# Order of the expert loop: gate products before linear products, a two-part activation, output products before the branch

## The chip, the cores and the metric

The kernel runs as one program on one core of a Trainium2 chip. The metric is the device time of one execution in microseconds (us). The median of three runs of the kernel before is 1742.16 us (1737.1 to 1744.37).

Five engines of the core work side by side, each with its own instruction stream: PE (TensorE, matrix products; PEld is its loading of weights), DVE (VectorE), ACT (ScalarE), POOL (GpSimd) and SP (SyncE, which here issues the loads of weights). They wait for each other by semaphores. In an fp32 product the trace shows two matmul records and two weight loads for each matmul that the program writes.

## The reference

Two transformer blocks on 256 tokens of width 1024. The first block ends in a mixture of 32 experts, of which each token takes four. This part is what the change touches:

```python
def moe_ffn(h, w_router, b_router, w_gu, b_gu, w_dn, b_dn):
    logits = (h @ w_router + b_router).astype(jnp.float32)
    top_logits, top_e = lax.top_k(logits, TOP_K)
    top_w = jax.nn.softmax(top_logits, axis=-1).astype(h.dtype)
    ...
    def expert_block(args):
        xe, e = args
        gu = xe @ w_gu[e] + b_gu[e]
        x_glu = jnp.minimum(gu[:, :D_FF], SWIGLU_LIMIT)
        x_lin = jnp.clip(gu[:, D_FF:], -SWIGLU_LIMIT, SWIGLU_LIMIT)
        act = (x_lin + 1) * (x_glu * jax.nn.sigmoid(SWIGLU_ALPHA * x_glu))
        return act @ w_dn[e] + b_dn[e]
    ...
    y = jnp.zeros((T + 1, D), h.dtype).at[slot_tok].add(yb.reshape(n_slots, D) * slot_w[:, None])
    return y[:T]
```

All arrays are float32. The weights of one expert are 12 MB (8 MB `w_gu`, 4 MB `w_dn`), all 32 experts 384 MB.

## The kernel before

**The loop.** The experts run one after the other (`for e in range(NX)`), 64 places (`CAP`) per expert. In the schedule written by hand, each engine does its instructions in the order of the code. One turn of the loop is, on PE:

1. `overflow(e)` (L1109 on): every engine loads the number of tokens of expert e (`TENSOR_LOAD`, L1121) and branches (`COMPARE_BRANCH`, L1122). If there are more than 64, an extra block `block(1)` does a whole expert for the next 64 tokens with the same weights; a second branch (L1124) guards two more. In the run traced here only expert 17 takes the extra block. Else PE jumps over all three blocks.
2. `up` (L1052): the bias by a product with `btab` (L1057), then for each of 8 tiles of `w_gu` (k = 0 to 7, 1 MB each) two products into the gate's accumulator `pg` and two into the linear part's `pl` (L1062). Two products of 64 columns each run beside each other. The tile is then free (`ring.done`). The activation follows on DVE and ACT: `g = min(pg, 7)` (L1069), `s = sigmoid` on ACT (L1070), and `a` from `pl`, `g` and `s` in three steps on DVE (L1071 to L1073).
3. `pre_gather(e + 1)`: 48 small products (L1028) collect the next expert's tokens in `px`; ACT copies them to `xe` (L1031).
4. Two of the four output products of the last pair of experts (`scatter_steps`, L1101, `po` from `sw` and `yb`; DVE adds each to `y`, L1103). Two experts fill the two halves of one `yb`.
5. For odd e `turn_weights` (L1047): four transposes that turn the slot weights `pw`; DVE copies them to `sw` (L1049).
6. `turn_act` (L1076): four transposes of `a` into `pa` (L1079), and one copy on ACT to `aT` (L1081).
7. `down` (L1084): the bias (L1088), then 16 products of `aT` with the four tiles of `w_dn` (L1092) into `py`. For odd e, ACT and DVE copy `py` to `yb` (L1176).

**The loads.** Class `Ring` holds a list of all weight tiles in order of use (12 per expert) and a set of buffers of 1 MB. SP issues the load of a tile into the buffer that was freed first (L68). Eight semaphores tell of the landings in turn, so that eight loads at most are under way.

**Buffers.** `pg`, `pl`, `sw`, `aT`, `yb` and `py` have one buffer each, `ps_x` (for `px`, `pw`, `pa`) and `ps_o` (for `po`) two.

## Time and profile before

| | |
|---|---|
| median of three runs | 1742.16 us |
| the profiled execution | 1738.1 us, of which the span of the trace 1736.4 us |
| PE busy | 1564.3 us (90% of the span) |
| PEld busy | 953.9 us (55%) |
| DVE busy | 662.1 us (38%) |
| ACT busy | 440.2 us (25%) |
| POOL busy | 135.6 us (8%) |
| read from HBM | 529.19 MB, 306 GB/s over the span |
| mean granted clock of TensorE | 0.957 of full speed |

The experts begin at 321.87 us of the span and their last `down` ends at 1315.8 us; what stands before makes the routing, what comes behind is the second block. A time in the text is counted from the start of the span. The granted clock has two levels, 1.00 (2.4 GHz) and 0.5 (1.2 GHz); a figure between them is a mean over a stretch. A busy share is a mean over stages with different limits; what holds the experts is read from rows of the experts.

### The profile page before, as it was taken

To read this page: it belongs to the slowest core of one execution; us is meant where nothing else is said; L and a number is where in the kernel's file an instruction comes from. 1 tells how busy PE (TensorE), PEld (TensorE's weight loads), DVE (VectorE), ACT (ScalarE), POOL (GpSimd) and SP (SyncE) were. 2 spreads that over 40 slices of the span, in tenths; PEclk is the share of its full clock that TensorE was granted. 3 is DMA by queue.
4 is the path that set the end of the run, shared out by engine and by line. 5 is a ranking of instruction groups with operands and counts; after the bars stand their busy time and mean duration, and the time that the engine had idled before them with its cause. 6 is when DMAs were issued, how large, how long until landed. Compare 5 with 4: busy or idle time off the path is not lost. (4 is left out here: it accounts for less than half of the span.)

```text
span 1736.4 us, 25332 instructions
## 1 busy us (share of the span) xinstructions
PE 1564.3 (90%) x10281; PEld 953.9 (55%) x10281; DVE 662.1 (38%) x1336; ACT 440.2 (25%) x940; POOL 135.6 (8%) x186
## 2 busy tenths in 40 slices
PE   5999998689898889989898988989887999999997
PEld 2887778433333233333233333333344989899996
DVE  3656567312121121212122121212116676766665
ACT  3445444200000000000000000000003666455554
POOL 3125012100000000000000000000003300200000
PEclk8999999699999899999999999999988999999999
DMA  9725867799999999999599999999973544455552
GB/s 366 173 93 204 303 236 290 287 416 416 416 417 415 418 414 417 416 416 417 220 400 417 416 397 417 415 416 417 416 292 99 189 146 146 132 171 194 173 199 91
DMA packets 163434, 533.79 MB, mean 307 GB/s; under 512 B 15957, under 2 KB 84758, under 8 KB 127264
## 3 DMA queue, kind: packets, MB, share of 16 engines
q1 hardware_dynamic: 159986, 523.56, 77.8%
q0 software_dynamic: 2480, 6.79, 1.2%
q8 instruction: 146, 2.39, 0.6%
q10 hardware_dynamic: 766, 0.60, 0.1%
q14 instruction: 56, 0.46, 0.1%
HBM read 529.19 MB, written 1.71 MB: 306 GB/s over the span
## 5 line engine op out<-in xcount | busy, mean ns | idle before, releaser
L1062 PE MATMUL pge<-ring,xee 128*64 128x512 f32 x1024 | 305.3, 633 | 8.6 <-issue 8.6
L1062 PE MATMUL ple<-ring,xee 128*64 128x512 f32 x1024 | 303.3, 629 | 1.0 <-issue 1.0
L1069 DVE TENSOR_SCALAR ge<-pge 128x512 f32<-128x512 f32 x32 | 22.1, 692 | 638.5 <-issue 617.6
L393 DVE TENSOR_TENSOR wlo<-ring,whi 128x512 fp32r<-128x512 f32 x338 | 215.7, 698 | 78.6 <-ACT whi L390 77.2
L1092 PE MATMUL py<-ring,aTe 128*64 128x512 f32 x1024 | 226.8, 595 | 12.6 <-ACT aTe L1081 7.9
L1070 ACT ACTIVATE se<-ge 128x512 f32<-128x512 f32 x32 | 20.2, 631 | 689.3 <-DVE ge L1069 689.3
L390 ACT CAST whi<-ring 128x512 fp32r<-128x512 f32 x344 | 188.2, 620 | 23.2 <-issue 17.8
L1062 PEld LDWEIGHTS ple<-ring,xee 128*64 128x64 f32 x1024 | 97.1, 145 | 146.5 <-issue 141.6
L1062 PEld LDWEIGHTS pge<-ring,xee 128*64 128x64 f32 x1024 | 97.1, 145 | 141.0 <-issue 125.4
L1092 PEld LDWEIGHTS py<-ring,aTe 128*64 128x64 f32 x1024 | 70.7, 137 | 150.0 <-issue 125.1
L1057 PE MATMUL pge<-btab,pick 96*64 96x512 bf16 x64 | 14.4, 403 | 80.6 <-PEq L1122 70.1
L1133 POOL DMA_DIRECT2D gains<-mod_dr x1 | 0.6, 604 | 932.0 <-DMA ring<-in_w_gu_dram 932.0
L1028 PEld LDWEIGHTS <-parts 128*128 128x128 bf16 x1584 | 49.1, 99 | 29.3 <-PE pge L1062 25.2
L1057 PEld LDWEIGHTS <-pick 96*64 96x64 bf16 x132 | 5.7, 107 | 107.9 <-issue 67.9
L1101 PE MATMUL poe<-yb,swe 128*128 128x512 f32 x128 | 62.8, 614 | 0.7 <-ACT yb L1176 0.7
L1028 PE MATMUL pxe<-onee,parts 128*128 128x64 bf16 x1536 | 51.5, 195 | 3.2 <-DVE rs L995 3.2
L1176 DVE COPY yb<-py 128x512 f32<-128x512 f32 x16 | 11.1, 692 | 105.7 <-PE py L1092 105.7
L443 PE MATMUL ua<-h3l,whi 128*128 128x256 f32 x176 | 49.9, 284 | 0.7 <-DVE h3l L1266 0.7
L444 PE MATMUL ua<-h3h,wlo 128*128 128x256 f32 x176 | 49.9, 284 | 0.0
L442 PE MATMUL ua<-h3h,whi 128*128 128x256 f32 x176 | 49.8, 283 | 0.0
L444 PE MATMUL uv<-h3h,wlo 128*128 128x256 f32 x176 | 49.2, 280 | 0.0
L442 PE MATMUL uv<-h3h,whi 128*128 128x256 f32 x176 | 49.1, 279 | 0.0
(581 smaller groups left out, 2960.7 us busy)
## 6 DMA issues: line engine op xcount, KB each, us to landing
ring<-in_w_gu_dram SPq DMA_DIRECT2D x256, 1024.0 KB, 15.7
ring<-in_w_dn_dram SPq DMA_DIRECT2D x128, 1024.0 KB, 16.4
ring<-in_w_in_dram SPq DMA_DIRECT2D x37, 1024.0 KB, 5.5
ring<-in_w_mod_dram SPq DMA_DIRECT2D x24, 1024.0 KB, 7.4
ring<-in_w_up_dram SPq DMA_DIRECT2D x22, 1024.0 KB, 5.0
ring<-in_w_down_dram SPq DMA_DIRECT2D x11, 1024.0 KB, 4.8
ring<-in_w_o_dram SPq DMA_DIRECT2D x4, 1024.0 KB, 7.3
ring<-in_w_out_dram SPq DMA_DIRECT2D x4, 1024.0 KB, 5.1
```

Source lines behind the costliest of these rows:

```text
L390: nc.scalar.copy(hq, wq)
L393: eng.tensor_tensor(out=lq, in0=wq, in1=hq.bitcast(F32), op=ALU.subtract)
L442: nc.tensor.matmul(ps, ah, bh, start=first, stop=False)
L443: nc.tensor.matmul(ps, ah, bl, start=False, stop=False)
L444: nc.tensor.matmul(ps, al, bh, start=False, stop=last)
L1028: nc.tensor.matmul(px[:, k, :], parts[:, t, q, k * P : (k + 1) * P], one[:, t, :], start=(t == 0 and q == 0 and k == 0), stop=(t == NT - 1 ...
L1057: nc.tensor.matmul((pg, pl)[ch // 2][64 * (ch % 2) : 64 * (ch % 2) + 64, :], sel, btab[:, ch * 512 : (ch + 1) * 512], start=True, stop=False)
L1062: nc.tensor.matmul((pg, pl)[ch // 2][64 * (ch % 2) : 64 * (ch % 2) + 64, :], xe[:, k, :], w[:, ch * 512 : (ch + 1) * 512], start=False, st ...
L1069: nc.vector.tensor_scalar_min(g, pg, 7.0)
L1070: nc.scalar.activation(out=s, in_=g, func=AF.Sigmoid, scale=1.702)
L1092: nc.tensor.matmul(at[c], aT[:, k % 4, 64 * (k // 4) : 64 * (k // 4) + 64], w[:, k % 2, c * 512 : (c + 1) * 512], start=False, stop=(k == ...
L1101: nc.tensor.matmul(po, sw[:, c, t * P : (t + 1) * P], yb[c], start=True, stop=True)
```

## The change

It changes the order of the expert loop; what is computed stays. In `up`, tiles 0 to 3 are used as before; tiles 4 to 7 are first used for the gate alone, then for the linear part, and are freed in this second pass. `g` is multiplied with `s` before the linear part is looked at, and the rest of the activation is done in two halves of 256 columns. `turn_act` transposes and copies each half by itself. The output products move from their place between `pre_gather` and `turn_act` to the end of the turn, behind `down` and so ahead of the next branch. `turn_weights` moves from the odd expert to the even one behind it, `slot_weights` behind it. In the extra block, the slot weights are computed and turned before the activation.

```diff
-        for k in range(KD):
+        def products(k, chunks):
             w = ring.get(("gu", e, k))
-            for ch in range(4):
+            for ch in chunks:
                 nc.tensor.matmul((pg, pl)[ch // 2][64 * (ch % 2) : 64 * (ch % 2) + 64, :], xe[:, k, :], w[:, ch * 512 : (ch + 1) * 512],
                                  start=False, stop=(k == KD - 1))
-            if release:
+            if release and 3 in chunks:
                 ring.done(("gu", e, k))
+        for k in range(KD // 2):
+            products(k, range(4))
+        for chunks in ((0, 1), (2, 3)):
+            for k in range(KD // 2, KD):
+                products(k, chunks)
...
         nc.scalar.activation(out=s, in_=g, func=AF.Sigmoid, scale=1.702)
-        nc.vector.tensor_scalar(out=a, in0=pl, scalar1=7.0, scalar2=-7.0, op0=ALU.min, op1=ALU.max)
-        nc.vector.scalar_tensor_tensor(out=a, in0=a, scalar=1.0, in1=g, op0=ALU.add, op1=ALU.mult)
-        nc.vector.tensor_tensor(out=a, in0=a, in1=s, op=ALU.mult)
+        nc.vector.tensor_tensor(out=g, in0=g, in1=s, op=ALU.mult)
+        for c in (slice(0, 256), slice(256, 512)):
+            nc.vector.tensor_scalar(out=a[:, c], in0=pl[:, c], scalar1=7.0, scalar2=-7.0, op0=ALU.min, op1=ALU.max)
+            nc.vector.scalar_tensor_tensor(out=a[:, c], in0=a[:, c], scalar=1.0, in1=g[:, c], op0=ALU.add, op1=ALU.mult)
...
-        for j in range(4):
-            nc.tensor.transpose(pt[:, j, :], a[:, j * P : (j + 1) * P], ident)
         aT = mp.tile([P, 4, P], F32, tag="aT", name=f"aT{name}", bufs=1)
-        nc.scalar.copy(aT, pt)
+        for c in range(2):
+            for j in (2 * c, 2 * c + 1):
+                nc.tensor.transpose(pt[:, j, :], a[:, j * P : (j + 1) * P], ident)
+            nc.scalar.copy(aT[:, 2 * c : 2 * c + 2], pt[:, 2 * c : 2 * c + 2])
...
         def block(b):
             name = f"v{e}_{b}"
-            aT = turn_act(up(e, gather(e, b, name), name), name)
+            xe = gather(e, b, name)
+            slot_weights(pw[1], e, b, (0, 2))
+            a = up(e, xe, name)
+            sw = turn_weights(pw[1], name)
+            aT = turn_act(a, name)
             py = ps_o.tile([P, 512], F32, tag="o", name=f"py{name}")
             down(e, aT, [py[64 * c : 64 * c + 64, :] for c in range(2)])
-            slot_weights(pw[1], e, b, (0, 2))
             yb = mp.tile([P, 512], F32, tag="ybv", name=f"yb{name}")
             nc.scalar.copy(yb, py)
-            scatter(turn_weights(pw[1], name), [yb, yb], name)
+            scatter(sw, [yb, yb], name)
...
     for e in range(NX):
-        odd = e % 2
+        odd, last_one = e % 2, e == NX - 1
         overflow(e)
 
-        one = select(e + 1, 0, f"e{e + 1}") if e + 1 < NX else None
-        if odd:
-            slot_weights(pw[0], e, 0, (1,))
+        one = None if last_one else select(e + 1, 0, f"e{e + 1}")
+        if odd or not e:
+            slot_weights(pw[0], e, 0, (1,) if odd else (0, 2))
         act = up(e, xs_.pop(e), f"e{e}", release=True)
 
-
         pre_gather(e + 1, one)
-        next(spread, None)
-        next(spread, None)
-        if odd:
+        if last_one:
+            run(spread)
             sw = turn_weights(pw[0], f"e{e}")
-        if e == NX - 1:
+        elif not odd and e:
+            sw = turn_weights(pw[0], f"e{e}")
+            spread = scatter_steps(sw, yb, f"e{e}")
+        act_T = turn_act(act, f"e{e}")
+        if not odd and e:
+            slot_weights(pw[0], e, 0, (0, 2))
+        if last_one:
             last_tables()
-        act_T = turn_act(act, f"e{e}")
-        if odd and e + 1 < NX:
-            slot_weights(pw[0], e + 1, 0, (0, 2))
-        if e == NX - 1:
             ring.pump()
...
         down(e, act_T, [py[c][rows[c], :] for c in range(2)], release=True)
+
+        next(spread, None)
+        next(spread, None)
         if odd:
             yb = [mp.tile([P, 512], F32, tag=f"yb{c}", name=f"yb{e}_{c}") for c in range(2)]
             for c in range(2):
                 (nc.scalar.copy, nc.vector.tensor_copy)[c](yb[c], py[c])
-            spread = scatter_steps(sw, yb, f"e{e}")
+    spread = scatter_steps(sw, yb, f"e{e}")
```

On PE, the end of expert 6's turn before (`py` is what `down` writes, `ring` a weight tile):

```order
L1092 MATMUL py_0_7843<-ring_7124,aTe_7841 64x512
L1092 MATMUL py_1_7844<-ring_7124,aTe_7841 64x512
L1092 MATMUL py_0_7843<-ring_7124,aTe_7841 64x512
L1092 MATMUL py_1_7844<-ring_7124,aTe_7841 64x512
L1121 TENSOR_LOAD counts
L1122 COMPARE_AND_BRANCH
```

and the same place of PE with the change (`poe` is an output product, `yb` and `swe` the last pair's outputs and turned slot weights):

```order
L1101 MATMUL py_0_7921<-ring_7195,aTe_7910 64x512
L1101 MATMUL py_1_7922<-ring_7195,aTe_7910 64x512
L1110 MATMUL poe_7949<-yb_0_7302,swe_7907 128x512
L1110 MATMUL poe_7952<-yb_1_7303,swe_7907 128x512
L1133 TENSOR_LOAD counts
L1134 COMPARE_AND_BRANCH
```

Two output products of 128 columns now stand between the last products of `down` and the branch; this holds from expert 2's turn on.

On PE, the products of `up` of expert 6 for tiles 4 to 7 before (`pge` the gate's accumulator, `ple` the linear part's):

```order
L1062 MATMUL pge_7717<-ring_6602,xee_7189 64x512 x2
L1062 MATMUL ple_7718<-ring_6602,xee_7189 64x512 x2
L1062 MATMUL pge_7717<-ring_7088,xee_7189 64x512 x2
L1062 MATMUL ple_7718<-ring_7088,xee_7189 64x512 x2
L1062 MATMUL pge_7717<-ring_7094,xee_7189 64x512 x2
L1062 MATMUL ple_7718<-ring_7094,xee_7189 64x512 x2
L1062 MATMUL pge_7717<-ring_7100,xee_7189 64x512 x2
L1062 MATMUL ple_7718<-ring_7100,xee_7189 64x512 x2
```

and with the change:

```order
L1062 MATMUL pge_7787<-ring_6656,xee_7260 64x512 x2
L1062 MATMUL pge_7787<-ring_7157,xee_7260 64x512 x2
L1062 MATMUL pge_7787<-ring_7163,xee_7260 64x512 x2
L1062 MATMUL pge_7787<-ring_7169,xee_7260 64x512 x2
L1062 MATMUL ple_7788<-ring_6656,xee_7260 64x512 x2
L1062 MATMUL ple_7788<-ring_7157,xee_7260 64x512 x2
L1062 MATMUL ple_7788<-ring_7163,xee_7260 64x512 x2
L1062 MATMUL ple_7788<-ring_7169,xee_7260 64x512 x2
```

The last tile is touched three product pairs earlier, and four pairs of linear products stand behind its gate product.

On DVE, the activation of expert 6 before (`ae` is `a`, `se` is `s`):

```order
L1069 TENSOR_SCALAR ge_7771<-pge_7717 128x512
L1071 TENSOR_SCALAR ae_7773<-ple_7718 128x512
L1072 SCALAR_TENSOR_TENSOR ae_7773<-ae_7773,ge_7771 128x512
L1073 TENSOR_TENSOR ae_7773<-ae_7773,se_7772 128x512
L1103 TENSOR_TENSOR y<-poe_7830,y 128x512
```

and with the change:

```order
L1076 TENSOR_SCALAR ge_7841<-pge_7787 128x512
L1078 TENSOR_TENSOR ge_7841<-ge_7841,se_7842 128x512
L1080 TENSOR_SCALAR ae_7843<-ple_7788 128x256
L1081 SCALAR_TENSOR_TENSOR ae_7843<-ae_7843,ge_7841 128x256
L1080 TENSOR_SCALAR ae_7843<-ple_7788 128x256
L1081 SCALAR_TENSOR_TENSOR ae_7843<-ae_7843,ge_7841 128x256
L1049 COPY swe_7907<-pwe_7902 128x512
```

Behind the linear part's last product stand four instructions of 256 columns instead of three of 512. The built program holds one more wait: the transposes of the second half wait for ACT's copy of the first half out of the same tile `pa`.

## Rows read from the trace of the kernel before

**Rows 1.** Windows: us, busy by engine, granted clock, DMA share, GB/s.
```profile
439.30:800.06 360.76, 324.36 (x1920) 129.93 (x1921) 70.51 (x144) 25.18 (x42) 0.00 (x0) 0.95 1.02 416
469.03:497.56 28.53, 25.96 (x162) 10.83 (x163) 6.75 (x14) 2.39 (x4) 0.00 (x0) 1.00 1.02 417
557.75:585.80 28.05, 25.52 (x160) 10.39 (x160) 5.02 (x10) 1.81 (x3) 0.00 (x0) 1.00 1.02 416
893.50:1254.27 360.77, 325.38 (x1921) 133.27 (x1922) 70.57 (x144) 25.18 (x42) 1.16 (x2) 0.95 1.01 413
```
**Rows 2.** Waits of PE, 439.30 to 1254.27: us in total, times, longest.
```profile
PE pge L1057 <- PEq L1122: 57.4, 26, 2.4
```
**Rows 3.** Timeline of PE round one branch: start, us, instructions, idle before.
```profile
880.46 1.96 PE L1101 MATMUL poe<-yb,swe 128*128 128x512 f32 x4
...
884.03 7.09 PE L1092 MATMUL py<-ring,aTe 128*64 128x512 f32 x32 [0.39 <-ACT aTe L1081]
893.50 0.41 PE L1057 MATMUL pge<-btab,pick 96*64 96x512 bf16 x2 [2.38 <-PEq L1122]
```
**Rows 4.** Lines of branch and last products: ns min/median/max, first to last start, us.
```profile
L1121 PEldq TENSOR_LOAD <-counts x1: 311/311/311, 886.7 to 886.7; - x1
L1122 PEldq COMPARE_BRANCH  x32: 82/6046/6250, 317.6 to 1276.2; - x32
L1092 PE MATMUL py<-ring,aTe x22: 592/592/592, 886.2 to 890.5; 128*64 128x512 f32 x22
L1028 PE MATMUL pxe<-onee,parts x21: 242/242/242, 316.8 to 317.9; 128*128 128x64 bf16 x21
```
**Rows 5.** Windows: granted clock behind a branch and, last, behind a short gap.
```profile
893.50:897.50 4.00, 4.00 (x14) 1.60 (x16) 0.00 (x0) 0.00 (x0) 0.00 (x0) 0.57 1.00 416
...
1510.04:1514.00 3.96, 3.96 (x34) 3.96 (x35) 2.86 (x8) 2.19 (x6) 3.04 (x4) 1.00 0.78 258
```
**Rows 6.** Timeline: the short gap of the row before, in the second block.
```profile
1510.04 0.39 PE L442 MATMUL ps_w_gla_branch<-sg_hi,whi 128*128 128x256 f32 x1 [1.22 <-DVE tgg L814]
```
**Rows 7.** Timeline of PE, expert 14: linear part's end to `down`.
```profile
908.50 1.05 PE L1062 MATMUL ple<-ring,xee 128*64 128x512 f32 x4
...
914.02 7.09 PE L1092 MATMUL py<-ring,aTe 128*64 128x512 f32 x32 [0.40 <-ACTq L1122]
```
**Rows 8.** Timeline of ACT: a copy in expert 14, and one of 256 columns.
```profile
911.09 0.59 ACT L1031 COPY xee<-pxe 128x512 f32<-128x512 f32 x1 [0.95 <-PE pxe L1028]
...
1337.96 0.37 ACT L1309 COPY fx<-ps_fq 128x256 f32<-128x256 f32 x1 [1.41 <-PE ps_fq L444]
```
**Rows 9.** Loads of tile 7 of experts 17 and 31: issue, and landing behind.
```profile
L68 SPq DMA_DIRECT2D ring<-in_w_gu_dram x1: 327/327/327, 810.3 to 810.3; - x1
...
DMA to landing us min/median/max: 19.9/19.9/19.9
...
L68 SPq DMA_DIRECT2D ring<-in_w_gu_dram x1: 327/327/327, 1261.8 to 1261.8; - x1
...
DMA to landing us min/median/max: 19.0/19.0/19.0
```
**Rows 10.** The first load issued after the extra block's pause.
```profile
L68 SPq DMA_DIRECT2D ring<-in_w_gu_dram x1: 332/332/332, 867.1 to 867.1; - x1
```
**Rows 11.** Timeline of PE in expert 17's extra block.
```profile
841.09 1.03 PE L1062 MATMUL plv<-ring,xev 128*64 128x512 f32 x4
...
845.88 8.78 PE L1092 MATMUL pyv<-ring,aTv 128*64 128x512 f32 x32 [0.40 <-ACT aTv L1081]
...
856.13 3.87 PE L1101 MATMUL pov<-ybv,swv 128*128 128x512 f32 x8 [0.88 <-DVE swv L1049]
863.07 0.53 PE L1057 MATMUL pge<-btab,pick 96*64 96x512 bf16 x2 [3.08 <-PEq L1124]
```
**Rows 12.** Timeline of PE, expert 31: after its branch, and its `down`.
```profile
1287.99 0.59 PE L1057 MATMUL pge<-btab,pick 96*64 96x512 bf16 x1 [5.19 <-issue]
...
1308.69 7.09 PE L1092 MATMUL py<-ring,aTe 128*64 128x512 f32 x32 [0.40 <-ACT aTe L1081]
```

More of the change, by code (lines that the diff above doesn't have):

```diff
@@ L1144 @@
     pre_gather(0, first)
-    slot_weights(pw[0], 0, 0, (0, 2))
+    yb, sw = None, None
     spread = iter(())
     for e in range(NX):
-        odd = e % 2
+        odd, last_one = e % 2, e == NX - 1
         overflow(e)
-        one = select(e + 1, 0, f"e{e + 1}") if e + 1 < NX else None
-        if odd:
-            slot_weights(pw[0], e, 0, (1,))
+        one = None if last_one else select(e + 1, 0, f"e{e + 1}")
+        if odd or not e:
+            slot_weights(pw[0], e, 0, (1,) if odd else (0, 2))
         act = up(e, xs_.pop(e), f"e{e}", release=True)
         pre_gather(e + 1, one)
-        next(spread, None)
-        next(spread, None)
-        if odd:
+        if last_one:
+            run(spread)
             sw = turn_weights(pw[0], f"e{e}")
-        if e == NX - 1:
+        elif not odd and e:
[5 more added lines that the diff above has]
+        if last_one:
             last_tables()
-        act_T = turn_act(act, f"e{e}")
-        if odd and e + 1 < NX:
-            slot_weights(pw[0], e + 1, 0, (0, 2))
-        if e == NX - 1:
             ring.pump()
```

## The prediction

> **What bounds the kernel now.** I first read the windows of the experts. Twelve experts take 360.76 us and a later twelve 360.77, so 30.06 us each; PE is busy for 90% of that and the 16 DMA engines for all of it, at 413 to 416 GB/s [rows 1]. An expert's twelve tiles are 12.58 MB, which is 30.2 to 30.5 us at that rate. So two limits lie on top of each other. PE gives the time as long as tiles landed ahead of their use, and the transfers give it once that lead is used up; the rows of a shorter PE turn must be held against 30.2 us before any gain is booked.
>
> Next I read what PE loses in a turn. A turn at the full clock throughout takes 28.05 us (even expert) or 28.53 (odd) [rows 1]; the mean is 1.8 above. The waits name the largest loss in a turn: 26 gaps at the branch, 57.4 us together, 2.2 each [rows 2]. The timeline shows one: `down` ends, 2.38 us pass, the next expert's bias starts [rows 3]. The lines of the branch say why. PE's sequencer reaches the branch early (its load of the count starts at 886.7) and the branch itself takes 6.05 us in the median. The array has work for part of that: at 886.7 some 18 of `down`'s records have not started (22 are in the window, four of them already running). In front of expert 0 the same window holds 21, although those have only 64 columns and are done in a fourth of the time [rows 4]. So the sequencer's lead is a number of instructions, not a time: 4.45 us here (891.12 - 886.67), against 6.83 from the load of the count to the next product.
>
> The gap costs more than itself. In the 4 us behind this one the granted clock is 0.57 of full, so 3.4 us at the lower level (1.2 GHz), a loss of 1.7 us [rows 5]. By my count 18 of 30 gaps of 2.0 to 2.4 us are followed by such a stretch; no gap of at most 1.28 us is. One of 1.22 us is shown, with the full clock behind it [rows 5, 6]. Full-clock turn plus one such stretch is about the mean.
>
> **The change, part by part.**
>
> *Output products in front of the branch.* Nothing is added or removed, two matmuls (four records) move. Four records took 1.96 us with the tail of the last one, 0.43 each without it; 32 records of `down` took 7.09, 0.214 each [rows 3]. If the lead is a count, its last four records now last 4 x (0.43 - 0.214) = 0.86 us longer. The gap falls from 2.2 to about 1.4. What hides the branch is still only what stands in the queue. DVE's adds, formerly among the activation's steps, run beside the gap. 1.4 lies between 1.28 (never a lower clock) and 2.0; I take it as harmless, since it is nearer to the former. The saving is thus 0.86 per turn for the gap, and up to 1.7 in those turns that now lose it to the clock.
>
> *Gate first, activation in two parts.* PE issues the same products. What changes is the chain from the linear part's end to `down`. In expert 14 the linear part ends at 909.55 (908.50 + 1.05) and `down` starts at 914.02 [rows 7]: 4.47 us, of which 1.71 are output products, which leave; 2.76 would be left. With the change, ACT's queue sets the chain: its copy of the next expert's tokens starts 1.54 us behind the linear part's end and takes 0.59; then comes the first half's copy, 0.37 as for another copy of 256 columns [rows 8]; the second half's transposes wait for that copy, as they write the same `pa`, and then their own copy follows. With hand-overs that is 3.55. An even expert (which now also turns the weights, in that shadow) has 0.8 more than 2.76; an odd one had 3.2 by the same sum and keeps it. So I charge 0.4 us per expert, between 0 (ACT's copies are early enough) and 0.8. Freed products no longer hide this; the work that did so now stands at the branch.
>
> *Tiles 4 to 7.* They are freed up to 2.6 us later (three pairs of 0.86), which costs nothing while 17 buffers serve at most eight transfers under way. But tile 7 is first touched 2.6 us earlier, and 4.29 us of products stand behind its landing (one pair, then four): that much of lead is given up.
>
> *The extra block.* Its `up` cannot end before the tile lands that it shares with expert 17. Below.
>
> Together a turn of PE at full clock is 28.3 - 0.86 + 0.4 = 27.9 us, 2.2 less than now. Over 32 experts that would be 69 us, but it is less than the 30.2 us of the transfers. So PE runs into the landings, and they set the sum.
>
> **The sum, from landings.**
> (a) Expert 17's tile 7 is issued at 810.3 and lands at 830.2 [rows 9], now and with the change, since the queue is full throughout. 17 turns would give PE 37 us; it gets what this landing leaves. The extra block's linear part ends at 842.12 now (841.09 + 1.03) [rows 11]; bound by the landing it ends at 830.2 + 0.86 + 3.43 = 834.5: -7.6.
> (b) In the block, 3.76 us lie between that end and `down` (845.88) [rows 11]. With two steps of the activation in halves, and half of the transposes done meanwhile, I take 2.2: -1.5. `down` took 8.78 there, against 7.09 at the full clock [rows 3, 11]; a shorter wait leaves the clock: -1.7. 1.47 us from its end to the output products become 0.75, as the weights have been turned: -0.7. Expert 17's own products start at 863.07 - 11.5 = 851.6.
> (c) The transfers pause in the block, since its tiles stay held. The first load behind it, at 867.1 [rows 10], comes at 855.6, and all later landings are 11.5 earlier. Expert 31's tile 7, issued at 1261.8 and landed at 1280.8 [rows 9], lands at 1269.3. PE alone would reach it sooner: 851.6 + 14 x 27.9 + 5 (a stall as below) + 14 = 1261. The point at which PE decides instead is a turn of 28.5.
> (d) The rest is PE's: + 4.29 (linear part) = 1273.6, + 4.2 to `down` (3.9 now, + 0.4) = 1277.8, + 7.09 = 1284.9. Now it is 1315.8 (1308.69 + 7.09) [rows 12]. So -31.
> (e) Waiting for tiles can itself lower the clock, as gaps of 2 us do; at 1.7 us each, in half of the cases, at two places (expert 17, expert 31), I give back 3 (with rounding): -28.
> What stands behind the experts, 420.6 us to the span's end, is untouched: nothing of its order moves and its loads follow earlier ones.
>
> The profiled execution took 1738.1 us, so 1710 in its terms; the median of the runs lies 4.1 above it, so **1714**. Bounds: -39 if both clock losses fail to appear and the pause of the transfers shortens more; -18 if PE's stall in front of expert 31's first products (5.19 us, 'issue': the sequencer waits for nothing shown [rows 12]) grows or returns at more branches, as code moves, and clock losses hit each turn partly. Main case: 1703 to 1724.
>
> **Rivals.**
> *R1, slower: the gap stays.* If the branch's time starts when the array is drained rather than when the sequencer reaches it, longer products in front of it hide nothing. Against it: the lead of 18 records in both shapes [rows 4]. The gap then stays at 2.2, the clock losses too, and each turn pays 0.4 for the activation whose cover was moved away: 30.06 + 0.4. Expert 17 is reached 6.4 later, the block gives 3.9 back, 14 further turns cost 5.6: +8. If the even turns that now escape the lower clock lose it too, up to +17. Middle +12: 1754. It decides from a gap that stays above 2.0. Chance 0.12.
>
> *R2: the clock falls at the activation instead.* Between the linear part and `down` PE now has small gather products, transposes and waits in a row, and no output products among them. For it: in the extra block, where only transposes and a wait of 2.41 us stand there, `down` ran at 8.78 instead of 7.09 [rows 11]. Against: the gather products stay, and single waits are about 1 us. Then a turn is 27.9 + 1.7 = 29.6, the gain 0.5 per turn; with the block's -4 that is -4 to -18, in the middle -12: 1730. Chance 0.14.
> The Trainium skill, "TensorE: Matmul & The Clock Gate", section "Part 4: PE-mode transpose", says that transposes in TensorE's transpose mode do not count as busy for the clock as products do. By that rule this rival gains weight, and R2's time is what it would give; the slow `down` in the extra block agrees with it, but the wait there would do as well.
>
> *R3: transfers go faster once nothing holds them*, beyond -39: 0.04. That the order does not change as written is excluded by the rows of the instruction order above.
>
> **How the numbers follow.** Forecast 0.70 at 1714 (1703 to 1724), R1 0.12 at 1754, R2 0.14 at 1730, R3 0.04. The range 1702 to 1733 holds the main case and most of R2. About 0.5% (8.7 us) is what a measurement can tell from no change. Faster by more than that: 0.66 of the main case and R3, R2 for the most part: 0.80. Within: 0.09, a part of R2, of the main case and of R1's low end. Slower: 0.11.
>
> **What would show it.** In the profile of the changed kernel: the gap at the branch at about 1.4 us, and a granted clock of 1.00 in the first 4 us of most experts; PE's waits naming landings of tiles 6 and 7 in `up`, from about the tenth expert; the extra block's end at 851.6 and the next load at 855.6; expert 31's `down` ending between 1285 and 1288; DMA share at 1 throughout. Wrong if the gap stays at 2 (R1), if products behind the activation run at 0.5 (R2), if no wait for a landing appears although PE's turn is near 30 (then PE still sets the time), or if the second half's transposes wait far more than 1 us for ACT's copy.

## The result, and the profile after

The changed kernel takes 1709.92 us (median of four runs, 1709.14 to 1711.24) against 1740.23 for the kernel before (a fourth run, 1738.3, stands beside the three that gave 1742.16): a ratio of 0.9823, 95% interval 0.9804 to 0.9841, some 30 us or 1.8% faster. The profiled execution took 1709.96 us, its span is 1708.2 us. Forecast were 1714 (1702 to 1733).

Windows of the changed kernel come first (us, busy time of PE, PEld, DVE, ACT and POOL with counts, granted clock, DMA share, GB/s): twelve experts' time of before for comparison, one even and one odd turn, and 4 us behind a branch.

```profile
439.30:800.06 360.76, 326.06 (x1964) 122.11 (x1961) 73.28 (x168) 26.44 (x54) 0.00 (x0) 0.99 1.02 416
496.36:524.54 28.18, 26.32 (x162) 9.78 (x163) 6.63 (x17) 1.96 (x4) 0.00 (x0) 1.00 1.02 416
524.54:552.35 27.81, 25.68 (x158) 10.25 (x158) 5.58 (x13) 2.45 (x5) 0.00 (x0) 1.00 1.02 417
524.54:528.54 4.00, 4.00 (x22) 1.77 (x24) 0.61 (x4) 0.00 (x0) 0.00 (x0) 1.00 1.03 410
```

The clock of the stretch went from 0.95 to 0.99 [rows 1], and behind a branch from 0.57 to 1.00 [rows 5]. A full-clock turn takes 28.18 or 27.81 us, mean 28.0, where 27.9 was forecast. The transfers are as busy as before. Now PE's waits over the experts (us in total, times, longest):

```profile
...
PE pae L1089 <- ACT aTe L1090: 19.8, 32, 0.8
PE pge L1062 <- DMA ring<-in_w_gu_dram: 8.3, 8, 1.4
```

Between 439.30 and 1254.27, the stretch of [rows 2], the two branch rows read so:

```profile
PE pge L1057 <- DVEq L1134: 18.7, 13, 1.4
...
PE pge L1057 <- PEq L1134: 10.8, 9, 1.3
```

29.5 us in 22 gaps are 1.34 each (before: 2.2, and 57.4 us in 26); three more, of 1.2 us each, end on a copy by DVE. Two new rows have appeared in the first list. The transposes of the second half wait for ACT's copy, 0.6 us each, as the built order said. And PE waits for landed weights, which it never did before. Between 630 and 822 us (experts 11 to 16) this is the first row of the waits:

```profile
PE pge L1062 <- DMA ring<-in_w_gu_dram: 7.3, 7, 1.4
```

The timeline of PE shows where: in expert 12, ahead of the gate's products of tiles 6 and 7, then the linear part runs without a stop.

```profile
677.20 1.08 PE L1062 MATMUL pge<-ring,xee 128*64 128x512 f32 x4 [1.11 <-DMA ring<-in_w_gu_dram]
679.68 1.08 PE L1062 MATMUL pge<-ring,xee 128*64 128x512 f32 x4 [1.41 <-DMA ring<-in_w_gu_dram]
680.59 3.60 PE L1062 MATMUL ple<-ring,xee 128*64 128x512 f32 x16
```

The extra block of expert 17 (rows of before: [rows 11]) and the end of expert 31 ([rows 12]), from the same view:

```profile
833.07 3.60 PE L1062 MATMUL plv<-ring,xev 128*64 128x512 f32 x16
...
837.75 0.41 PE L1089 MATMUL pav<-ident,av 128*128 128x128 f32 x2 [0.49 <-DVE av L1081]
838.68 0.44 PE L1089 MATMUL pav<-ident,av 128*128 128x128 f32 x2 [0.52 <-ACT aTv L1090]
...
839.29 7.03 PE L1101 MATMUL pyv<-ring,aTv 128*64 128x512 f32 x32
847.01 3.89 PE L1110 MATMUL pov<-ybv,swv 128*128 128x512 f32 x8 [0.69 <-ACTq L1136]
854.98 0.41 PE L1057 MATMUL pge<-btab,pick 96*64 96x512 bf16 x2 [4.07 <-PEq L1136]
...
856.80 1.92 PE L1062 MATMUL ple<-ring,xee 128*64 128x512 f32 x4
...
1272.04 1.08 PE L1062 MATMUL pge<-ring,xee 128*64 128x512 f32 x4 [0.95 <-DMA ring<-in_w_gu_dram]
...
1280.24 7.04 PE L1101 MATMUL py<-ring,aTe 128*64 128x512 f32 x32
```

Expert 31's `down` ends at 1287.28 instead of 1315.78, that is 28.5 us earlier; behind it 420.9 us are left (before: 420.6). The whole difference lies in the experts.

### The profile page after: what moved, and what is told of

It reads as the page before. It is cut to its first block, busy times and chain, and to the rows that moved or that the text cites. A ratio compares the mean times of both kernels' runs of the same rounds, so it can differ in the third digit from the quotient of the medians.

```text
span 1708.2 us, 25401 instructions
## 1 busy us (share of the span) xinstructions
PE 1549.9 (91%) x10281; PEld 926.7 (54%) x10281; DVE 669.3 (39%) x1402; ACT 443.4 (26%) x973; POOL 135.4 (8%) x186
## 5 line engine op out<-in xcount | busy, mean ns | idle before, releaser
L1062 PE MATMUL pge<-ring,xee 128*64 128x512 f32 x1024 | 264.1, 605 | 12.9 <-DMA ring<-in_w_gu_dram 8.3
L1062 PE MATMUL ple<-ring,xee 128*64 128x512 f32 x1024 | 263.2, 605 | 6.3 <-issue 6.3
L1062 PEld LDWEIGHTS ple<-ring,xee 128*64 128x64 f32 x1024 | 84.5, 139 | 154.7 <-issue 152.7
L1062 PEld LDWEIGHTS pge<-ring,xee 128*64 128x64 f32 x1024 | 84.1, 140 | 142.3 <-issue 112.5
L1112 DVE TENSOR_TENSOR y<-poe,y 128x512 f32<-128x512 f32 x64 | 44.1, 691 | 263.2 <-PE poe L1110 263.1
L443 PE MATMUL uv<-h3l,whi 128*128 128x256 f32 x176 | 49.1, 279 | 0.0
```

The lines of the kernel that those rows point to most:

```text
L443: nc.tensor.matmul(ps, ah, bl, start=False, stop=False)
L1062: nc.tensor.matmul((pg, pl)[ch // 2][64 * (ch % 2) : 64 * (ch % 2) + 64, :], xe[:, k, :], w[:, ch * 512 : (ch + 1) * 512], start=False, st ...
L1112: nc.vector.tensor_tensor(out=sl, in0=po, in1=sl, op=ALU.add)
```

## The experiments

Nine kernels ran, one profile of each. The first four separate the parts of the change and test the reason given for the gap; the next three test whether landings or PE set the time; the last two try what the rows suggested. A word for what follows: a stall of the kind 'issue' is a stop of PE for which the list of waits names no semaphore.

### Only the changed order of the loop

```diff
 (the changed kernel, with up, turn_act and block of the kernel before)
-        for chunks in ((0, 1), (2, 3)):
-            for k in range(KD // 2, KD):
-                products(k, chunks)
+        for k in range(KD):
+            ... all four chunks, then ring.done(("gu", e, k))
```

> The changed order of the loop alone: output products in front of the branch, weights turned in the even expert; `up`, the activation, `turn_act` and the extra block as in the kernel before. Theory (the branch gap is the source, the landings take it over): gap at the branch 1.2 to 1.5 us, granted clock 0.97 or more over the span, and a turn at full clock of 27.5 to 28.1 us. No tile is freed later, so expert 17's tile 7 lands at about 830.2 us again (832.1 in the changed kernel), and only 1.71 us of products stand behind it instead of 4.29: the extra block's linear part ends at about 832 (836.7 in the changed kernel), and the total is 1704 to 1714, no slower than the whole change. Rival (gate first and the halved activation bring a good part of the gain): 1720 to 1730.

Measured: 1715.49 us (1709.61 to 1718.62), ratio 0.9854 (0.9833 to 0.9874). That is 26 of the 30 us. The profiled execution is the shortest of the four, 6 us below the median, so its rows flatter it. PE's waits from 439.30 to 1254.27:

```profile
PE pge L1057 <- DVEq L1122: 20.1, 14, 1.4
PE pae L1079 <- DVE ae L1073: 17.7, 27, 0.9
PE pge L1057 <- PEq L1122: 13.0, 11, 1.3
```

The gap is as short as with the whole change (33.1 us in 25), the clock 0.99. So the source is the output products' new place. The median lies just above the range given, and "no slower than the whole change" did not hold: the median is 5.6 us above it. I had put a turn at 27.5 to 28.1, but without the output products between gather and transposes PE now waits 0.66 us for DVE's third step, 27 times, and a turn is 28.4 (28.31 and 28.55 for experts 6 and 7). An odd turn is 0.74 shorter with the halved activation. That this makes the 5.6 us is likely but not shown, since the run that was profiled took no longer than the changed kernel.

### Only gate first, the activation and the extra block

```diff
 (the kernel before, with up, turn_act and block of the changed kernel; the loop's order stays)
+        for k in range(KD // 2):
+            products(k, range(4))
+        for chunks in ((0, 1), (2, 3)):
+            for k in range(KD // 2, KD):
+                products(k, chunks)
```

> The complement: gate first, activation and `turn_act` in two parts and the extra block's new order, with the loop's order of before (output products between the gather and the transposes). Theory: the gap stays at 2.0 to 2.4 us and the clock falls behind it in about 18 of 30 turns; the output products cover ACT's copies again, so a turn gains 0.3 to 0.7 us (29.4 to 29.8); tile 7 of expert 17 lands 2 us later than before and bounds the extra block; with the block's own gain of 3: 1720 to 1732. Rival A (the two-part activation costs 0.4 per turn even here): 1738 to 1748. Rival B (it is the source of the whole gain): 1708 to 1714.

Measured: 1733.86 us (1730.24 to 1739.53), ratio 0.9959 (0.9937 to 0.998): 7 us faster, a miss by 2 us of the range, between theory and rival A. The window of experts 4 to 15 shows the clock of before:

```profile
439.30:800.06 360.76, 324.58 (x1920) 132.55 (x1918) 73.25 (x168) 27.03 (x54) 0.00 (x0) 0.95 1.02 416
```

PE's waits over the experts show that the second transposes wait for ACT although the output products stand ahead of them:

```profile
PE pae L1089 <- ACT aTe L1090: 16.5, 31, 0.8
```

A turn gained nothing, where 0.3 to 0.7 us were expected. `down` starts 0.18 us later in it than before (19.44 instead of 19.27 us into an odd turn without a fall of the clock, 19.01 instead of 18.83 in an even one). What is left is the extra block, which brings expert 17's own products forward by 3.75 us (859.32 instead of 863.07), near the 3.9 of the forecast's step (b). Expert 17's tile 7 was expected 2 us later and to bound the block; it landed at 830.6 (before: 830.2), and PE did not wait for it. The rest of the 7 us lies in experts 18 to 31, where stalls of the 'issue' kind fell differently; it is within what runs of this kernel differ by. So the two halves of the change are worth 26 and 7 by themselves, and 30 when both are made: the halved activation pays in a turn only where the output products no longer cover it.

### Filler in front of the branch

```diff
         down(e, act_T, [py[c][rows[c], :] for c in range(2)], release=True)
+        if 1 < e < NX - 1:
+            for c in range(2):
+                nc.tensor.matmul(ps_o.tile([P, 512], F32, tag="o", name=f"fill{e}_{c}"), ident, yb[c], start=True, stop=True)
```

> The kernel before with two more products of 128 columns (four records) in front of the branch in experts 2 to 30; nobody reads their result. Their work is added, nothing is moved. Theory (the sequencer's lead is a number of instructions, and a gap below 1.5 us leaves the clock alone): gap 1.3 to 1.5 us, a branch of 6.0 to 6.2 us, no half clock behind gaps in experts 3 to 30; each turn pays 1.72 us for the products, gets 0.86 back in the gap and about 1.0 from the clock: 1728 to 1745. Rival (the branch's time counts from the drained array): gap 2.2 us, clock as before, 29 x 1.72 = 50 us more: 1785 to 1795.

Measured: 1741.19 us (ten runs, 1735.99 to 1745.89), ratio 0.9998 (0.9985 to 1.0011). Four more records in each of 29 turns made no difference that the runs show. PE's timeline at expert 10's end:

```profile
650.41 1.98 PE L1175 MATMUL fill<-yb,ident 128*128 128x512 f32 x4
653.47 0.41 PE L1057 MATMUL pge<-btab,pick 96*64 96x512 bf16 x2 [1.07 <-PEq L1122]
```

The window of the 4 us behind it:

```profile
653.47:657.47 4.00, 4.00 (x22) 1.75 (x24) 0.00 (x0) 0.00 (x0) 0.00 (x0) 1.00 1.03 420
```

The gaps among PE's waits from 439.30 to 1254.27:

```profile
PE pge L1057 <- PEq L1122: 26.1, 22, 1.5
```

The gap is 1.2 us in the mean, 1.0 less than before; the branch itself is not shorter (6.09 us in the median of that stretch, 6.04 before). So the time is counted from the sequencer's arrival, which leads by a number of instructions, and long products at the end stretch that lead: the rival on which the slower case R1 rested is gone. A count over the traces says the same: in the kernel before, the changed one, the run with the loop's order alone and this one, 18 records start behind the load of the count in 30 of 31 branches (17 in one), and they last 4.4 us in the first and 5.5 us in the other three. By my count of the timeline, none of the gaps at the outer branch is followed by the lower clock from expert 3 on. 1.72 us of work per turn are paid by 1.0 from the gap and the rest from the clock.

### Gate first for the last two tiles alone

```diff
-        for k in range(KD // 2):
+        for k in range(KD - 2):
             products(k, range(4))
         for chunks in ((0, 1), (2, 3)):
-            for k in range(KD // 2, KD):
+            for k in range(KD - 2, KD):
```

> The changed kernel with gate first for tiles 6 and 7 alone instead of tiles 4 to 7. Theory (the transfers and the products behind the last landing bound the extra block): tiles are freed up to 0.86 us later than in the kernel before instead of 2.57, so expert 17's tile 7 lands 830.2 to 831.5 us (832.1 in the changed kernel), and 2.57 us of products stand behind it instead of 4.29. The extra block's linear part ends 1.7 to 3.5 us earlier, at 833 to 835; activation and transposes as in the changed kernel to 0.3 us; total 1705 to 1709, that is 1 to 4 below the changed kernel. Rival (the landings are not what bounds the block): 1709 to 1712, no different.

Measured: 1707.92 us (1706.21 to 1709.1), ratio 0.9806 (0.979 to 0.9823). The interval overlaps that of the whole change; the profile decides more sharply. PE in the extra block:

```profile
830.89 1.89 PE L1062 MATMUL plv<-ring,xev 128*64 128x512 f32 x8
...
835.72 7.03 PE L1101 MATMUL pyv<-ring,aTv 128*64 128x512 f32 x32
...
852.54 0.64 PE L1057 MATMUL pge<-btab,pick 96*64 96x512 bf16 x2 [5.20 <-PEq L1136]
```

The linear part ends at 832.78, 3.9 us earlier than in the changed kernel, just ahead of the 833 to 835 of the theory: expert 17's tile 7 landed at 829.9 (832.1 there), and 2.57 us of products follow instead of 4.29. PE no longer waits at that tile; its last wait is for expert 16's tile 7 (1.39 us, until 799.98 instead of 802.10), where the same two numbers apply. Of the 3.9, 1.1 are lost again at once to a longer gap behind the block.

### Smaller loads, in the changed kernel and in the one before

```diff
-            self.nc.sync.dma_start(out=t, in_=src)
+            w = {"gu": 1856, "dn": 896}.get(key[0], shape[-1])
+            self.nc.sync.dma_start(out=t[..., :w], in_=src[..., :w])
...
-                ... w[:, ch * 512 : (ch + 1) * 512]
+                ... w[:, ch * 448 : ch * 448 + 512]
-                ... w[:, k % 2, c * 512 : (c + 1) * 512]
+                ... w[:, k % 2, c * 384 : c * 384 + 512]
```

In the changed kernel:

> The changed kernel, in which each weight tile of the experts is loaded only in part (1856 of 2048 columns of `w_gu`, 896 of 1024 of `w_dn`); the products keep their number and size and read overlapping columns, so the result is not the reference's. An expert's loads fall from 12.58 MB to 11.27 MB, 27.1 us at 416 GB/s, less than PE's turn of 28.0. Theory (the landings bound experts 11 to 16 and the extra block): the waits for tiles in `up` vanish, about 12 us of PE's waiting in experts 11 to 16, the extra block's linear part ends at 823 to 827 instead of 836.7, expert 31 saves 1 us: total 1694 to 1701. If the branch is also quicker with the queues less full, the gap shows it and the total is lower by that. Rival (landings bound nothing, PE's own work does): 1706 to 1711.

Measured: 1693.78 us (1692.75 to 1696.11), ratio 0.9739 (0.9724 to 0.9754), 16 us below the changed kernel and just below the 1694 to 1701 given. No wait for a tile is left. The gaps at the branch among PE's waits from 439.30 to 1254.27, and the branch's own line (ns, min/median/max), are as in the changed kernel (1.34 us each, 6.11 us in the median):

```profile
PE pge L1058 <- PEq L1135: 15.3, 12, 1.6
PE pge L1058 <- DVEq L1135: 15.2, 11, 1.4
```

```profile
L1135 PEldq COMPARE_BRANCH  x27: 82/6097/6502, 459.2 to 1239.2; - x27
```

The timeline of PE in the extra block:

```profile
820.81 3.60 PE L1063 MATMUL plv<-ring,xev 128*64 128x512 f32 x16
...
841.58 0.41 PE L1058 MATMUL pge<-btab,pick 96*64 96x512 bf16 x2 [2.93 <-PEq L1137]
```

The linear part ends at 824.41, 12.3 us earlier, within the range of the theory, but not by 12 us of waiting: the waits for tiles in experts 11 to 16 were 7.3 us. 2.6 us were there at expert 11's start (634.07 instead of 636.62), ahead of any wait for a tile; 2.4 us are in no single row. The gap behind the block gives 1.1 more (2.93 instead of 4.07), and expert 17 starts at the full clock (1.7). Gap and branch are unchanged, so a quicker branch is not the source. That landings hold the changed kernel back in experts 11 to 16 and at expert 31 is thus shown; they cost it at most these 16 us.

In the kernel before:

> The same smaller loads in the kernel before (result not the reference's). Theory (before, PE's turn of 30.06 us sets the time and the landings run ahead by 12 to 25 us): no wait for a tile was there to be removed, so 1734 to 1744, apart from a quicker branch, which the gap would show. Rival (loads bound the kernel before as well): 1720 or less, with the gap and the clock as they were.

Measured: 1724.15 us (1715.76 to 1727.62), ratio 0.992 (0.9905 to 0.9935). 16 us faster, where I had written at most 6: a miss. But the rows that the rival needed are not there either, since gap and clock did not stay. The gaps among PE's waits from 439.30 to 1254.27, in the profiled execution (the shortest of five):

```profile
PE pge L1058 <- PEq L1123: 48.6, 26, 2.3
```

The window of the same stretch, and below it the branch's line with the duration of one in ns (min, median, max):

```profile
439.30:1254.27 814.97, 736.29 (x4458) 298.26 (x4460) 164.93 (x336) 58.75 (x98) 1.16 (x2) 0.97 0.95 371
```

```profile
L1123 PEldq COMPARE_BRANCH  x27: 82/5673/6206, 433.9 to 1228.5; - x27
```

The branch takes 5.67 us in the median instead of 6.04, the gap 1.87 instead of 2.2, and the clock is 0.97 instead of 0.95: fewer gaps are followed by the lower clock. Why the branch is quicker here stays open. The smaller loads alone do not make it so: in the changed kernel with the same loads it took 6.10 us, with the transfers at 0.94 of their time against 0.95 here. No wait for tiles was removed, as there was none. How much of the 16 us each of these makes is not settled; the profiled execution lies 8 us below the median.

### No shared buffer for the second transposes

```diff
-        pt = ps_x.tile([P, 4, P], F32, tag="x", name=f"pa{name}")
         for c in range(2):
+            pt = (ps_x, ps_o)[c].tile([P, 4, P], F32, tag="xo"[c], name=f"pa{name}_{c}")
```

> The changed kernel with gate first for tiles 6 and 7 alone (as in the run e4_gate_first_two), and the second half's transposes go into a buffer of the other pool, so that they don't wait for ACT's copy of the first half. Theory: the wait of the second transposes for ACT (18.8 us in 32 times there) falls below 6 us, a turn at full clock from 28.0 to 27.4 us; but the landings bound the extra block and expert 31, so of 32 x 0.6 = 19 us only 1 to 3 arrive: 1705 to 1707. Rival (PE's own turn is what counts): 1690 to 1697.

The diff is against the run e4_gate_first_two. Measured: 1706.67 us (1703.76 to 1706.91), ratio 0.9803 (0.9789 to 0.9816). The wait of 0.52 is gone; PE's timeline in expert 6 has all four transposes in a row:

```profile
510.20 0.66 PE L1089 MATMUL pae<-ident,ae 128*128 128x128 f32 x4 [0.21 <-ACT xee L1031]
```

In its place PE waits more often for ACT's copy of the tokens (9.7 us in 30 times, 3.1 in 15 before this edit). A full-clock turn falls to 27.5 or 27.7 us. Over 32 turns that would be some 12 us, and 1.3 arrive (1707.92 to 1706.67). The rival 1690 to 1697 is excluded. That PE reaches the landings sooner and waits there accounts for a part: the waits for tiles rise from 2.4 to 5.1 us. The stalls of the kind 'issue' in `up`'s products rise too, from 10.6 to 12.6 us.

### The inner branch first

```diff
         with tc.If(n > CAP):
-            block(1)
             with tc.If(n > 2 * CAP):
                 block(2)
                 block(3)
+            block(1)
```

> The changed kernel with one move: inside the extra block's branch, the inner branch (for more than 128 tokens) stands ahead of `block(1)` instead of behind it, so that PE no longer jumps behind the block's last products. Theory (from the extra block on, each us saved there arrives at the end, since the loads resume that much earlier): the gap of 4.07 us in front of expert 17's own products falls below 1.5 and no half clock follows it (1.7); at the block's start the jump's time lies partly under the last products of expert 16, and the wait of 0.95 us there grows to 1.5 to 3 us. Net 2.5 to 5 us earlier at expert 17's own start and at the first load behind the pause, and as much at the end: 1705 to 1707.5. Rival (PE and the landings in experts 18 to 31 hide it): 1709 to 1711.

Measured: 1707.25 us (1706.46 to 1710.07), ratio 0.9802 (0.9785 to 0.9819). The gap of 4.07 us at the block's end is gone entirely, but the time came back at its start, as PE's timeline shows:

```profile
817.99 0.83 PE L1028 MATMUL pxv<-onev,parts 128*128 128x64 bf16 x23 [1.64 <-DVE onev L871]
823.37 1.52 PE L1028 MATMUL pxv<-onev,parts 128*128 128x64 bf16 x25 [4.54 <-issue]
```

PE stops for 4.54 us in the middle of the gather, with nothing in the profile to wait for. Expert 17's own products start at 855.05 (854.98 in the changed kernel). The expected 2.5 to 5 us at that point did not come; the median, 2.7 below the changed kernel, lies with the theory, but the profiled run, the slowest of the five (1710.07), does not show why. I take the theory as not shown here. The trace does show what moved while PE stood: besides the loads, a block on the DMA queue `q8` of the kind `instruction`. It is there from 820.80 to 822.00 (packets, MB, share), and none from then to 823.30:

```profile
q8 instruction: 1, 0.02, 5.7%
```

PE goes on 1.4 us behind the end of this block (821.97). That the time behind the inner branch was the loading of code, and came back where PE next needed code, agrees with this.

### All three edits

> All three edits on the changed kernel: gate first for tiles 6 and 7 alone, the second half's transposes in a buffer of the other pool, the inner branch first. Theory: the gains of e7_two_psum (3 to 4 us below the changed kernel) and of e8 (2.5 to 5) add up, since both lie in the extra block: 1701 to 1704. Rival (one of the two is then hidden): 1705 to 1707.

Measured: 1703.73 us (1701.68 to 1705.38), ratio 0.9778 (0.9761 to 0.9795), 6 us below the changed kernel, within the range of the theory, and the lowest median of the versions with the full result (its interval overlaps that of the run with no shared buffer, 0.9789 to 0.9816). Why the gains add up is not shown: in the profiled run, the slowest of five, expert 17's own products start at 853.62, only 1.4 us ahead of the changed kernel's.

## Why the prediction was right, step by step

The sign, the chain of causes (a shorter gap, no lower clock behind it, then PE held by landings) and the size (-30 measured, -28 forecast) held. That the profiled execution came out at 1709.96, with 1710 forecast, is luck, as shown below. The forecast of the median, 1714, added 4.1 us by which the median of before lay above its profile; the changed kernel's median lies at its profile. The terms of the sum against the rows:

| step | forecast | measured |
|---|---|---|
| gap at the branch | 1.4 us | 1.34 |
| full-clock turn of PE | 27.9 us | 28.0 |
| linear part's end to `down`, even expert | 3.55 us | 3.74 (expert 6: 510.72 to 514.46) |
| (a) extra block's linear part ends | 834.5 | 836.67 |
| (b) from there to `down` | 2.2 us | 2.62 |
| (b) `down` there | 7.09 us | 7.03 |
| (b) its end to the output products | 0.75 us | 0.69 |
| (b) expert 17's own products | 851.6 | 854.98 |
| (c) first load behind the pause | 855.6 | 858.8 |
| (c) expert 31's tile 7 lands | 1269.3 | 1272.0 |
| (d) linear part's end to `down`, expert 31 | 4.2 us | 3.69 |
| (d) expert 31's `down` ends | 1284.9 | 1287.28 |
| (e) allowance for the clock | 3 us | see below |

**The gap and the clock.** The lead of the sequencer as a number of instructions was the central step; the filler run shows it alone. The gap of 1.4 us did not cost the clock. In half of the turns the gap is now ended by DVE (1.44 us each, odd experts' ends): its two adds and the copy of `yb` stand ahead of its own branch, and PE's first product behind the branch waits for it. I had let DVE's adds "run beside the gap"; they set it there, for some 0.2 us.

**The landings.** PE met them in experts 11 to 16 ("from about the tenth"), on tiles 6 and 7, and the smaller loads took these 7.3 us of waiting away. The comparison with 69 us in the prediction does not hold, though. It set a turn at full clock (27.9) against a mean (30.06) that also holds expert 9's stall of 4.6 us, and "full-clock turn plus one such stretch is about the mean" counts a lower clock in every turn, where 18 of 30 had one. The stalls stayed. With no wait for a tile, in the run with smaller loads, experts 4 to 15 take 28.7 us each, 1.35 less than before, and the whole kernel is 47 us faster than before. So of some 47 us, 30 arrive. The sum itself went by landings and did not use the 69.

**What failed: the landing taken as fixed, and "freed later costs nothing".** Expert 17's tile 7 landed 2 us later (issued at 812.2, 19.9 to landing) where I had kept 830.2. The transfers are busy without a pause from expert 0 to there: from the landing of expert 2's first tile to this one it is 477 us in both kernels (353.2 to 830.2, 355.2 to 832.1). So the delay arises in expert 0, and it has two parts.

The smaller part is the change's. In expert 0 the buffers are full; the load of expert 1's second `w_dn` tile waits for tile 4 of expert 0, which gate first frees only in the linear pass. SP's issue of that load, in the kernel before and in the changed one:

```profile
L68 SPq DMA_DIRECT2D ring<-in_w_dn_dram x1: 373/373/373, 336.9 to 336.9; - x1
DMA to landing us min/median/max: 7.8/7.8/7.8
```

```profile
L68 SPq DMA_DIRECT2D ring<-in_w_dn_dram x1: 374/374/374, 339.3 to 339.3; - x1
DMA to landing us min/median/max: 7.5/7.5/7.5
```

It is issued 2.4 us later, while two earlier loads are still under way (they land at 340.8 and 343.3). The tile lands 3.5 us behind the one ahead of it instead of 2.6, so 0.9 us of the delay stay (0.2 are made up behind it). I had looked at the number of transfers under way and not at the place where there are few.

The larger part, 1.3 us, is there before that. Expert 1's tile 7 is issued at the same time in both, and takes longer to land in the changed kernel. Before and changed:

```profile
L68 SPq DMA_DIRECT2D ring<-in_w_gu_dram x1: 328/328/328, 333.4 to 333.4; - x1
DMA to landing us min/median/max: 6.1/6.1/6.1
```

```profile
L68 SPq DMA_DIRECT2D ring<-in_w_gu_dram x1: 328/328/328, 333.3 to 333.3; - x1
DMA to landing us min/median/max: 7.5/7.5/7.5
```

What makes this part is open. It is of the size by which the kernels differ anyway: expert 17's tile 7 lands at 832.1, 830.6 (activation alone) and 829.6 (inner branch first) with gate first for four tiles, at 829.9, 831.2 and 830.7 with gate first for two, at 830.2, 830.7 and 830.6 (kernel before, order of the loop alone, filler) with none. So the earlier landing in the run with two tiles is not shown to come from the buffers.

**What was missing: the inner branch.** Its jump costs 4.07 us now and 3.08 before [rows 11]. I had carried the 3.08 over. The line of this branch in both kernels, before and changed (the longest is the one of expert 17):

```profile
L1124 PEldq COMPARE_BRANCH  x2: 203/1946/3688, 858.9 to 862.8; - x2
```

```profile
L1136 PEldq COMPARE_BRANCH  x2: 203/2466/4728, 849.8 to 854.7; - x2
```

It took 4.73 us instead of 3.69; the block now ends while loads are still landing (until 855.4; before, they had ended at 852.7 and the branch ran at 859 to 863). This 1.0 us is the second part of what was lost. The half clock behind it (856.80: 1.92 us for four records, 1.02 at the full clock) is no new loss: it stood behind the gap of 3.08 as well (863.81: 1.92).

**What the allowance stood for.** 3 us were held back for clock losses at waits for tiles. These waits stayed at 1.4 us or less and the clock at 1.00. Instead expert 17's own products started 3.4 us later than forecast: 2.2 from the end of the linear part, 0.4 from there to `down`, 1.0 from the inner branch, less 0.1 elsewhere. Of that, 2.4 are left at the end of expert 31's `down`, where the activation took 0.5 less than I had charged. The forecast of the total is so close because two errors cancel.

**PE against landings in experts 18 to 31.** I had let the landings lead by 8 us at expert 31. PE waited there 0.95 us only. The 14 turns of experts 17 to 30 took 406 us (854.98 to 1261.03), 29.0 each, against 28.0 at the full clock. Most of the difference lies in three of them: the half clock at expert 17's start (29.5), and stalls of the kind 'issue' in experts 26 and 30, with the lower clock behind each (34.5 and 32.8). One such stall was in the sum. PE's waits between 882 and 1254 us:

```profile
PE pge L1062 <- issue: 4.1, 1, 4.1
PE ple L1062 <- issue: 2.2, 1, 2.2
```

**The rivals.** R1 needed a gap above 2.0: it is 1.34. R2 needed the lower clock behind the activation: `down` takes 7.03 or 7.04 and the clock is 1.00, with gather, transposes and two waits in a row. No run here shows the rule of the Trainium skill that was weighed there ("TensorE: Matmul & The Clock Gate", "Part 4: PE-mode transpose"). Four to eight transposes among products changed nothing.

## What to carry to other kernels

A jump costs the array what its instruction takes less the work already handed over, and that lead is a number of instructions (18 records here): put the longest instructions last in front of it, and the same count covers more time (here 0.43 instead of 0.21 us each for the last four, 0.9 us per branch, and the clock with it). Before adding up what an engine saves, hold its turn against the stream that feeds it, and compare like with like: a mean turn holds stalls, which this reordering did not take away. Here some 47 us of PE's time became 30, as the loads need 30.2 us for a turn. And a buffer that is freed later is free of charge only while enough loads are under way; look for the place where they are few, since a delay there (here 0.9 us) stays in every later landing.

## What the runs showed of the hardware that I had not expected

- Every long jump of PE and every stall of the kind 'issue' in the experts ends a fixed time behind a block of 16 KB (0.02 MB) on the DMA queue `q8` of the kind `instruction`. A count over the eleven traces: all 350 branches above 1 us (outer and inner) end 1.3 to 1.6 us behind the landing of such a block, and PE goes on 1.2 to 1.6 us behind one in all 56 stalls above 1 us. For expert 13's stall in the changed kernel (699.5 to 703.63) the block is there from 701.20 to 702.40 (packets, MB, share), and none from then to 703.60:

```profile
q8 instruction: 1, 0.02, 5.6%
```

  So these stalls are waits for code as far as traces can tell; no run took the block away. They come four to eight times in the experts of every kernel here, at other experts when the code is changed (before: experts 0, 9, 22 and 31; changed: 0, 13, 26 and 30). The Trainium skill, "Runtime: NRT & Kernel Launch", section "Instruction fetch mechanics", says that a taken branch to a target outside of the fetched window forces a fetch by DMA before execution goes on. The block inside each of the 350 branches agrees with it.
- The inner branch takes longer while loads are still landing: 3.4 to 3.8 us where they had ended (before, activation alone, filler), 4.0 and 4.7 where they ended 4 and 6 us behind its start (order of the loop alone, changed kernel), 5.9 and 6.0 where they ended 6 and 7 us behind it (gate first for two tiles, no shared buffer). The outer branch does not follow the load in this way: 6.04 us with the transfers at 0.99 of their time, but 5.67 at 0.95 in one kernel and 6.10 at 0.94 in another.
- A gap of 1.44 us or less at the branch was never followed by the lower clock in the changed kernel, by my count of its 28, unless a stall came in between (expert 26); of those of 2.0 to 2.4 us before, 18 of 30 were, at 1.7 us each. By these numbers the 0.9 us of a shorter gap bring about 1.0 more by the clock.
